# Loading the first tile of a rotary-embedding kernel in four pieces ahead of its tables, and storing the last tile in four pieces

## The chip, the core and the metric

The kernel runs on one core of one Trainium2 chip. The metric is the time of one execution on the device in microseconds (us), as the median of several executions. A profile is a separate, recorded execution with its own time; the span is the part of it from the first to the last instruction.

The core has a matrix engine (TensorE, "PE" in the profile), a vector engine (VectorE, "DVE"), a scalar engine (ScalarE, "ACT"), GpSimd ("POOL") and SyncE ("SP"). In this kernel SP only issues transfers. The transfers themselves are carried by 16 DMA engines. An engine whose name ends in q in the profile, such as SPq, is its instruction queue: issuing a transfer or waiting there is not counted as busy time.

## The reference

The reference applies a rotary position embedding to x of shape 16 x 512 x 1024, in float32. Each row of 1024 is 16 heads of 64, and each head is cut into two halves of 32. The cosine and sine tables have one row of 32 for each of the 512 positions.

```python
x = x.reshape(batch, seq, num_heads, head_dim)
x1, x2 = x[..., :half_dim], x[..., half_dim:]
cos, sin = cos[None, :, None, :], sin[None, :, None, :]
rotated = np.concatenate([x1 * cos - x2 * sin, x1 * sin + x2 * cos], axis=-1)
```

So 32 MiB are read, 32 MiB are written, and the arithmetic is two products and a sum for each element.

## The kernel before

**Tiling.** Two batches make a tile: 64 partitions for each, 128 in all, with R = 8 consecutive positions (rows of 1024) on each partition. A tile is 128 partitions by 8192 numbers, 4 MiB, with 32 KB on each partition. There are NT = 8 tiles. The pool `xin` holds NB = 5 of them, and the result is written over the tile itself, so that a tile's buffer is loaded, rotated in place and stored from.

**Tables.** The tables are loaded as `tabs` (64 partitions, 256 numbers for sine and 256 for cosine; lines 61 and 62). Three matrix products (lines 88 to 90) spread them over the 128 partitions into PSUM, as `sns_ps` (sine with both signs) and `cos_ps`, and ScalarE copies them to SBUF as `sns` and `cost` (lines 94 and 95). VectorE reads the PSUM copies and GpSimd reads `sns`.

**One tile (`compute`).** Rows 0 and 1 are single rows: the swapped halves are multiplied by the sine into B (line 121; row 0 on GpSimd, row 1 on VectorE), the row by the cosine in place (line 131, VectorE), and the matrix engine adds the two through an identity matrix (lines 136 and 137), from where ScalarE copies the sum back into the tile (line 138). Rows 2 and 3, 4 and 5, 6 and 7 go as pairs: GpSimd makes T (line 126), VectorE makes the cosine product pp (line 142) and adds both into the tile (line 143).

**Order of the transfers.** The schedule is written by hand, and each engine runs its instructions in the order of the program. All transfers are issued by SP, on one queue: sine, cosine, the first tile in two halves of 2 MiB (lines 63 and 64), and tiles 1 to 4 whole (line 68). Then tiles 0, 1 and 2 are stored when they are done (line 148); tiles 5, 6 and 7 are loaded into the buffers that these stores free (line 68 again); tiles 3 and 4 are stored (line 152), then 5 and 6 (line 156), and the last tile in two halves (lines 157 and 158). A store waits for its rows on VectorE and ScalarE; the second half of the last tile waits for VectorE's last instruction.

```python
nc.sync.dma_start(out=tabs[:, 1], in_=sinv)
nc.sync.dma_start(out=tabs[:, 0], in_=cosv)
nc.sync.dma_start(out=x_tiles[0][:, :H], in_=xv[0][:, :H])
nc.sync.dma_start(out=x_tiles[0][:, H:], in_=xv[0][:, H:])
```

The full kernel follows.

Of the kernel before, what the change touches and what calls it, by code (L numbers as in the profile page):

```python
# [7 lines left out]
FP32 = mybir.dt.float32  # L8
# [4 lines left out]
def kernel(  # L13
# [8 lines left out]
    nc = tc.nc  # L22
    P = nc.NUM_PARTITIONS
    batch, seq, dim = x.shape
# [7 lines left out]
    R = seq // HP  # L32
    NT = batch // BP
# [5 lines left out]
    xv = x.rearrange("b (p r) d -> (b p) (r d)", r=R)  # L39
    xv = xv.rearrange("(t p) f -> t p f", p=P)  # L40
    ov = out.rearrange("b (p r) h d -> (b p) (r h d)", r=R)
    ov = ov.rearrange("(t p) f -> t p f", p=P)
    cosv = cos.rearrange("(p r) j -> p (r j)", r=R)
    sinv = sin.rearrange("(p r) j -> p (r j)", r=R)

    fixed = ctx.enter_context(tc.tile_pool(name="fixed", bufs=1))
    xin = ctx.enter_context(tc.tile_pool(name="xin", bufs=NB))
# [6 lines left out]
    ctx.enter_context(tc.manual_schedule())  # L54


    tabs = fixed.tile([HP, 2, R * half], FP32, name="tabs")
    x_tiles = [None] * NT
    x_tiles[0] = xin.tile([P, R * dim], FP32, name="x_sb")
    H = R * dim // 2  # L60
    nc.sync.dma_start(out=tabs[:, 1], in_=sinv)
    nc.sync.dma_start(out=tabs[:, 0], in_=cosv)
    nc.sync.dma_start(out=x_tiles[0][:, :H], in_=xv[0][:, :H])
    nc.sync.dma_start(out=x_tiles[0][:, H:], in_=xv[0][:, H:])

    def load(t):
        x_tiles[t] = xin.tile([P, R * dim], FP32, name="x_sb")
        nc.sync.dma_start(out=x_tiles[t], in_=xv[t])

    for t in range(1, NB):  # L70
        load(t)

# [4 lines left out]
        out=ident, in_=ident, compare_op=ALU.not_equal, fill=1.0,  # L77
# [35 lines left out]
    def compute(t):  # L113
        xt = x_tiles[t]
        ts = {}
        bs = {}

        for r in PEROWS:
            B = bpool.tile([P, dim], FP32, name="B")
            eng = nc.vector if r == PEROWS[-1] else nc.gpsimd  # L120
            eng.tensor_tensor(out=B, in0=swapped(xt, r, 1), in1=snsb(sns_ps if eng is nc.vector else sns, r, 1),  # L121
                              op=ALU.mult)
            bs[r] = B
        for r0 in PAIRS:
            T = tpool.tile([P, 2 * dim], FP32, name="T")
            nc.gpsimd.tensor_tensor(out=T, in0=swapped(xt, r0, 2), in1=snsb(sns, r0, 2), op=ALU.mult)  # L126
            ts[r0] = T

        for r in reversed(PEROWS):
            xr = view(xt, r, 1)  # L130
            nc.vector.tensor_tensor(out=xr, in0=xr, in1=cosb(cos_ps, r, 1), op=ALU.mult)  # L131
            for c in range(2):
                ps = prow.tile([P, dim // 2], FP32, name="ps")
                xc = xr[:, c * dim // 2:(c + 1) * dim // 2]
                bc = bs[r][:, c * dim // 2:(c + 1) * dim // 2]
                nc.tensor.matmul(out=ps, lhsT=ident, rhs=xc, start=True, stop=False)  # L136
                nc.tensor.matmul(out=ps, lhsT=ident, rhs=bc, start=False, stop=True)  # L137
                nc.scalar.copy(out=xc, in_=ps)  # L138
        for r0 in PAIRS:
            pp = ppair.tile([P, 2 * dim], FP32, name="pp")  # L140
            xr = view(xt, r0, 2)
            nc.vector.tensor_tensor(out=pp, in0=xr, in1=cosb(cos_ps, r0, 2), op=ALU.mult)  # L142
            nc.vector.tensor_tensor(out=xr, in0=ts[r0], in1=pp, op=ALU.add)  # L143

    for t in range(NB):
        compute(t)
        if t < NT - NB:
            nc.sync.dma_start(out=ov[t], in_=x_tiles[t])
    for t in range(NB, NT):
        load(t)  # L150
    for t in range(NT - NB, NB):
        nc.sync.dma_start(out=ov[t], in_=x_tiles[t])
    for t in range(NB, NT):
        compute(t)
        if t < NT - 1:
            nc.sync.dma_start(out=ov[t], in_=x_tiles[t])
    nc.sync.dma_start(out=ov[NT - 1][:, :H], in_=x_tiles[NT - 1][:, :H])
    nc.sync.dma_start(out=ov[NT - 1][:, H:], in_=x_tiles[NT - 1][:, H:])


# [33 lines left out]
```

## Time and profile before

| quantity | before |
|---|---|
| time, median of 3 runs | 164.61 us (164.56 to 164.94) |
| time of the profiled execution | 164.86 us |
| its span | 162.7 us |
| VectorE busy | 137.7 us (85%) |
| GpSimd busy | 127.1 us (78%) |
| TensorE busy (modelled ends) | 77.5 us (48%) |
| ScalarE busy | 21.0 us (13%) |
| packet time of the one data queue, as a share of 16 engines' span | 97.0% |
| bytes moved | 67.25 MB, 413 GB/s over the span |
| transfers issued by SP | 20 |

The busy times are sums over the span; the shares are averages over stages. The profile also shows for every transfer the time from its issue to its landing, and for stretches of the span the DMA engines' busy share. In the view by stretches a packet is counted whole in the stretch in which it ends, so that a share can be over 1.00 in one row and under it in the next. Besides, the trace holds a record of every packet of a transfer, with its start, its length in time and its bytes. A packet of a tile is one partition's share of a transfer: 32,768 bytes for a whole tile and 16,384 for a half.

### The profile page before, as it was taken

How to read it: one execution, taken by the hardware profiler on the slowest of the kernel's cores; microseconds unless marked ns; L12 is line 12 of the kernel's file. 1: busy time of each engine (PE TensorE's matmuls, PEld its weight loads, DVE VectorE, ACT ScalarE, POOL GpSimd, SP SyncE). 2: the span in 40 equal slices, each digit the busy share in tenths (PEclk: the TensorE clock that was granted, in tenths of full speed). 3: DMA queues.
4: the chain of work that ended last, by engine and by line, in shares of the span. 5: the costliest groups of instructions: out<-in, count | busy, mean ns of one | idle time of the engine just before them, and what ended most of it. 6: DMA issues, size and time to landing. Idle time of an engine off the chain costs nothing. (4 is left out here: it accounts for less than half of the span.)

```text
span 162.7 us, 575 instructions
## 1 busy us (share of the span) xinstructions
PE 77.5 (48%) x134; PEld 32.3 (20%) x134; DVE 137.7 (85%) x75; ACT 21.0 (13%) x35; POOL 127.1 (78%) x38
## 2 busy tenths in 40 slices
PE   2409910499019920894059701990089205990000
PEld 2204400243013400341024201330034002330000
DVE  1067999999999999999999999999999999999100
ACT  3200310013101210022002300121004100131000
POOL 1069999999998799959995999779995999590000
PEclk9999997559855995589557995699659975598555
DMA  4999989999899998999999999989989989999992
GB/s 101 387 447 467 435 387 500 403 395 508 387 403 371 443 459 387 475 427 403 467 413 411 467 411 427 475 387 459 443 387 459 443 387 492 411 411 415 439 427 121
DMA packets 2753, 67.25 MB, mean 413 GB/s; under 512 B 320, under 2 KB 448, under 8 KB 448
## 3 DMA queue, kind: packets, MB, share of 16 engines
q1 hardware_dynamic: 2752, 67.24, 97.0%
q14 instruction: 1, 0.01, 0.0%
HBM read 33.69 MB, written 33.55 MB: 413 GB/s over the span
## 5 line engine op out<-in xcount | busy, mean ns | idle before, releaser
L126 POOL TENSOR_TENSOR T<-x_sb,sns 128x2048 f32<-128x2048 f32 x24 | 108.3, 4532 | 10.4 <-DVE x_sb L143 10.4
L136 PE MATMUL ps<-x_sb,ident 128*128 128x512 f32 x64 | 44.4, 783 | 65.7 <-issue 41.4
L143 DVE TENSOR_TENSOR x_sb<-T,pp 128x2048 f32<-128x2048 f32 x24 | 54.9, 2287 | 3.4 <-POOL T L126 1.0
L142 DVE TENSOR_TENSOR pp<-x_sb,cos_ps 128x2048 f32<-128x2048 f32 x24 | 55.0, 2293 | 0.6
L137 PE MATMUL ps<-B,ident 128*128 128x512 f32 x64 | 40.1, 713 | 0.0
L138 ACT COPY x_sb<-ps 128x512 f32<-128x512 f32 x32 | 18.8, 586 | 121.7 <-PE ps L137 120.6
L136 PEld LDWEIGHTS ps<-x_sb,ident 128*128 128x128 f32 x64 | 15.1, 251 | 87.8 <-issue 81.0
L121 POOL TENSOR_TENSOR B<-x_sb,sns 128x1024 f32<-128x1024 f32 x8 | 18.8, 2350 | 8.3 <-DMA x_sb<-in_x_dram 8.3
L137 PEld LDWEIGHTS ps<-B,ident 128*128 128x128 f32 x64 | 15.4, 240 | 21.8 <-issue 21.8
L131 DVE TENSOR_TENSOR x_sb<-x_sb,cos_ps 128x1024 f32<-128x1024 f32 x16 | 18.8, 1218 | 0.5
L121 DVE TENSOR_TENSOR B<-x_sb,sns_ps 128x1024 f32<-128x1024 f32 x8 | 9.7, 1215 | 7.7 <-DMA x_sb<-in_x_dram 7.7
L88 PE MATMUL sns_ps<-tabs,sel 64*128 64x256 f32 x2 | 1.2, 696 | 3.1 <-DMA tabs<-in_sin_dram 3.1
L94 ACT ACT_TABLE_LOAD x1 | 1.3, 1283 | 0.7 <-PEq L175 0.7
L81 DVE COPY sel<-ident 64x64 f32<-64x64 f32 x1 | 0.2, 186 | 1.3 <-POOL ident L76 1.3
L88 PEld LDWEIGHTS sns_ps<-tabs,sel 64*128 64x128 f32 x2 | 0.5, 306 | 3.1 <-issue 3.1
L89 PE MATMUL sns_ps<-tabs,sel 64*128 64x256 f32 x2 | 1.1, 631 | 0.0
L90 PE MATMUL cos_ps<-tabs,sel 64*128 64x256 f32 x2 | 1.1, 631 | 0.0
L94 ACT COPY sns<-sns_ps 128x512 f32<-128x512 f32 x1 | 0.6, 586 | 3.2 <-PE sns_ps L89 3.2
L89 PEld LDWEIGHTS sns_ps<-tabs,sel 64*128 64x128 f32 x2 | 0.7, 333 | 0.2
L90 PEld LDWEIGHTS cos_ps<-tabs,sel 64*128 64x128 f32 x2 | 0.7, 333 | 0.2
L75 POOL MEMSET ident<- 128x128 f32 x1 | 0.2, 205 | 0.3 <-POOLq L175 0.3
L95 ACT COPY cost<-cos_ps 128x256 f32<-128x256 f32 x1 | 0.4, 373 | 0.3 <-PE cos_ps L90 0.3
(7 smaller groups left out, 1.1 us busy)
## 6 DMA issues: line engine op xcount, KB each, us to landing
x_sb<-in_x_dram SPq DMA_DIRECT2D x7, 4096.0 KB, 29.8
out_dram<-x_sb SPq DMA_DIRECT2D x7, 4096.0 KB, 27.5
x_sb<-in_x_dram SPq DMA_DIRECT2D x2, 2048.0 KB, 9.6
out_dram<-x_sb SPq DMA_DIRECT2D x2, 2048.0 KB, 10.1
tabs<-in_sin_dram SPq DMA_DIRECT2D x1, 64.0 KB, 2.2
tabs<-in_cos_dram SPq DMA_DIRECT2D x1, 64.0 KB, 2.3
```

The source lines that it names most:

```text
L88: nc.tensor.matmul(out=sns_ps[:, :, 1, :], lhsT=sel[:, 0, :], rhs=sin3, start=True, stop=True)
L89: nc.tensor.matmul(out=sns_ps[:, :, 0, :], lhsT=sel[:, 1, :], rhs=sin3, start=True, stop=True)
L90: nc.tensor.matmul(out=cos_ps.rearrange("p r j -> p (r j)"), lhsT=sel[:, 0, :], rhs=tabs[:, 0], start=True, stop=True)
L94: nc.scalar.copy(out=sns, in_=sns_ps)
L121: eng.tensor_tensor(out=B, in0=swapped(xt, r, 1), in1=snsb(sns_ps if eng is nc.vector else sns, r, 1), op=ALU.mult)
L126: nc.gpsimd.tensor_tensor(out=T, in0=swapped(xt, r0, 2), in1=snsb(sns, r0, 2), op=ALU.mult)
L131: nc.vector.tensor_tensor(out=xr, in0=xr, in1=cosb(cos_ps, r, 1), op=ALU.mult)
L136: nc.tensor.matmul(out=ps, lhsT=ident, rhs=xc, start=True, stop=False)
L137: nc.tensor.matmul(out=ps, lhsT=ident, rhs=bc, start=False, stop=True)
L138: nc.scalar.copy(out=xc, in_=ps)
L142: nc.vector.tensor_tensor(out=pp, in0=xr, in1=cosb(cos_ps, r0, 2), op=ALU.mult)
L143: nc.vector.tensor_tensor(out=xr, in0=ts[r0], in1=pp, op=ALU.add)
```

## The change

The order of the first transfers, the queue of the two tables and the cutting of the first load and of the last store change; arithmetic, tiles and buffers stay. The first tile is loaded ahead of the tables in four pieces of two rows each (128 partitions by 2048 numbers, 1 MiB, 8,192 bytes on each partition). The tables are issued by ScalarE, on its own queue. The last tile is stored in four pieces of the same size. There are 24 transfers instead of 20: 22 issued by SP and 2 by ScalarE.

```diff
+    x_tiles = [None] * NT
+    def load(t, pieces=1):
+        x_tiles[t] = xin.tile([P, R * dim], FP32, name="x_sb")
+        n = R * dim // pieces
+        for i in range(pieces):
+            nc.sync.dma_start(out=x_tiles[t][:, i * n:(i + 1) * n], in_=xv[t][:, i * n:(i + 1) * n])
+
+    def store(t, pieces=1):
+        n = R * dim // pieces
+        for i in range(pieces):
+            nc.sync.dma_start(out=ov[t][:, i * n:(i + 1) * n], in_=x_tiles[t][:, i * n:(i + 1) * n])
+
+    load(0, pieces=4)
     tabs = fixed.tile([HP, 2, R * half], FP32, name="tabs")
-    nc.sync.dma_start(out=tabs[:, 1], in_=sinv)
-    nc.sync.dma_start(out=tabs[:, 0], in_=cosv)
-    nc.sync.dma_start(out=x_tiles[0][:, :H], in_=xv[0][:, :H])
-    nc.sync.dma_start(out=x_tiles[0][:, H:], in_=xv[0][:, H:])
+    nc.scalar.dma_start(out=tabs[:, 1], in_=sinv)
+    nc.scalar.dma_start(out=tabs[:, 0], in_=cosv)
...
     for t in range(NB, NT):
         compute(t)
-        if t < NT - 1:
-            nc.sync.dma_start(out=ov[t], in_=x_tiles[t])
-    nc.sync.dma_start(out=ov[NT - 1][:, :H], in_=x_tiles[NT - 1][:, :H])
-    nc.sync.dma_start(out=ov[NT - 1][:, H:], in_=x_tiles[NT - 1][:, H:])
+        store(t, pieces=4 if t == NT - 1 else 1)
```

On the compute engines the order of instructions is the same as before. On ScalarE the two issues stand ahead of the activation-table load that was its first instruction. Transfers share eight completion semaphores in turn, and as these are dealt out anew, two loads get a wait that they did not have: the load of tile 3 waits for the landing of the sine table, and that of tile 4 for the landing of the first piece of tile 0.

More of the change, by code (lines that the diff above doesn't have):

```diff
@@ L54 @@
     ctx.enter_context(tc.manual_schedule())
-    tabs = fixed.tile([HP, 2, R * half], FP32, name="tabs")
[L58 to L63, printed above, removed]
-    nc.sync.dma_start(out=x_tiles[0][:, H:], in_=xv[0][:, H:])
-    def load(t):
-        x_tiles[t] = xin.tile([P, R * dim], FP32, name="x_sb")
-        nc.sync.dma_start(out=x_tiles[t], in_=xv[t])
+    x_tiles = [None] * NT
+    Q = 2 * dim
+    def load(t, pieces=1):
[8 more added lines that the diff above has]
+    load(0, pieces=4)
+    tabs = fixed.tile([HP, 2, R * half], FP32, name="tabs")
+    nc.scalar.dma_start(out=tabs[:, 1], in_=sinv)
+    nc.scalar.dma_start(out=tabs[:, 0], in_=cosv)
     for t in range(1, NB):
@@ L147 @@
         if t < NT - NB:
-            nc.sync.dma_start(out=ov[t], in_=x_tiles[t])
+            store(t)
     for t in range(NB, NT):
@@ L151 @@
     for t in range(NT - NB, NB):
-        nc.sync.dma_start(out=ov[t], in_=x_tiles[t])
+        store(t)
     for t in range(NB, NT):
         compute(t)
-        if t < NT - 1:
-            nc.sync.dma_start(out=ov[t], in_=x_tiles[t])
-    nc.sync.dma_start(out=ov[NT - 1][:, :H], in_=x_tiles[NT - 1][:, :H])
-    nc.sync.dma_start(out=ov[NT - 1][:, H:], in_=x_tiles[NT - 1][:, H:])
+        store(t, pieces=4 if t == NT - 1 else 1)
 _INS = ['x', 'cos', 'sin', 'num_heads']
```

## The prediction

> **What bounds the kernel.** I read the page's busy shares first, then the 40 slices and the queue.
>
> ```profile
> PE 77.5 (48%) x134; PEld 32.3 (20%) x134; DVE 137.7 (85%) x75; ACT 21.0 (13%) x35; POOL 127.1 (78%) x38
> ...
> DMA  4999989999899998999999999989989989999992
> ...
> q1 hardware_dynamic: 2752, 67.24, 97.0%
> ```
>
> No compute engine is above 85%, while the DMA engines are full in every slice but the first and the last. Next comes the order of SP's issues (start, length, line).
>
> ```profile
> 0.73 0.54 SPq L61 DMA_DIRECT2D tabs<-in_sin_dram  x1
> 1.33 0.57 SPq L62 DMA_DIRECT2D tabs<-in_cos_dram  x1
> 1.96 0.58 SPq L63 DMA_DIRECT2D x_sb<-in_x_dram  x1
> ...
> 146.89 0.33 SPq L157 DMA_DIRECT2D out_dram<-x_sb  x1
> 151.29 0.33 SPq L158 DMA_DIRECT2D out_dram<-x_sb  x1
> ```
>
> By the lines' own views the halves L157 and L158 land 9.8 and 10.3 us after issue, so at 156.7 and 161.6: 4.9 us apart, though issued 4.4 apart. The last half is not late because VectorE was: it stood in line. The wait view says the same of SP's end, and shows what compute waits for at the start:
>
> ```profile
> SPq L189 <- DMA out_dram<-x_sb: 10.0, 1, 10.0
> ```
> ```profile
> DVE B L121 <- DMA x_sb<-in_x_dram: 7.7, 1, 7.7
> ```
>
> Short stretches show the two edges (columns: stretch, length, five engines' busy time, clock, DMA share, GB/s).
>
> ```profile
> 2.00:2.50 0.50, 0.00 (x0) 0.00 (x0) 0.00 (x0) 0.01 (x1) 0.00 (x0) 1.00 0.34 115
> 2.50:3.00 0.50, 0.00 (x0) 0.00 (x0) 0.00 (x0) 0.00 (x0) 0.00 (x0) 1.00 0.54 96
> 3.00:3.50 0.50, 0.39 (x1) 0.42 (x2) 0.00 (x0) 0.00 (x0) 0.00 (x0) 1.00 2.36 510
> ...
> 159.50:160.00 0.50, 0.00 (x0) 0.00 (x0) 0.00 (x0) 0.00 (x0) 0.00 (x0) 0.50 0.32 131
> 160.00:160.50 0.50, 0.00 (x0) 0.00 (x0) 0.00 (x0) 0.00 (x0) 0.00 (x0) 0.50 0.08 33
> ```
>
> Between 2 and 3 us only tables move, with holes; between 3 and 160 the engines are full. The packet records are finer: the first packet of x starts at 3.19 us, 16 packets are in flight from then to 159.7, 15 engines are done by 160.3 and the last at 161.25. So the span is: the start of the x stream, plus the work of one DMA engine (4.2 MB), plus about 1.4 us from its last packet to the last instruction. Compute counts only where it makes that stream run dry.
>
> **Prices, from the packet records.** One packet holds its engine for 1.213 us at 32 KB, 0.611 at 16 KB, 0.046 at 1 KB (the tables) and 0.009 for a 4-byte completion. That is 0.0367 us per KB plus some 0.009 a packet, so 8 KB should take 0.310; a lone 8 KB instruction fetch at 83.5 us took 0.309. Each engine carries 8 packets of a 128-partition transfer and 4 of a table.
>
> **Part 1: the tables leave SP's queue.** Their issues fill 0.735 to 1.962, and x is now issued first. The sine table, issued at 0.735, had its first packet at 2.06; the first x packet, issued at 1.962, at 3.19: 1.2 to 1.3 us from issue to packet. So x can start at 2.06: **-1.13 us**. The bounds: if ScalarE's sine issue takes its turn ahead, x is where cosine was (issue 1.34, first packet 2.70): -0.49; if both go ahead, 0. ScalarE begins its first instruction at 0.733 in this trace and SP at 0.735, so the trace doesn't say who comes first if they must take turns; its back-to-back issues on one engine show no turns between two. I take the two as parallel and keep 0 as the far end.
>
> **Part 2: the tables' packets.** Before, they ran while x was still on its way; now they run beside it. An engine has 8 packets of 0.046 and 2 completions of 0.009: **+0.39 us** if the engine is full. The first x packets took 0.83 to 1.51 us instead of 0.611, some 0.8 us lost on each engine once; table packets might fit into that for nothing, so the other end is 0. I take the full price, since everywhere else in the stream an extra packet shows as time.
>
> **Part 3: quarters for halves**, twice. A tile costs an engine 32 packets of 0.310 instead of 16 of 0.611: 9.92 - 9.78 = 0.14. Two more completions with their gaps of 0.006: 0.03. Both tiles: **+0.34 us**. Between the two halves of the first tile the records show no hole, only the 0.015 us of a completion. The lower end is 0, as a smaller packet can't carry the same bytes cheaper. The upper: 8 KB fetches before the span took 0.42 to 0.55, so 0.11 more on 64 packets, +7 us; that is far off, on idle engines, and the fetch inside the stream gives 0.309.
>
> The Trainium skill speaks against this part. "DMA: Bandwidth & Descriptors", section "Anatomy of one DMA — SWDGE (gpsimd) path", gives each DMA some 2.0 us of fixed cost beside its bytes, which for four more DMAs would be an estimated +8 us. The rows above disagree for queued transfers, as the halves follow each other within 0.015 us; the page's figure is for another issue path and for a DMA by itself.
>
> **Part 4: earlier compute.** The first quarter (rows 0 and 1) should land near 2.06 + 0.8 + 8 x 0.31 + 0.35 = 5.7 instead of 9.5. Sine landed at 3.0 and VectorE could start 2.15 us later (three matrix products queued); with packets interleaved I put sine near 4.5 and VectorE's start near 6.7 instead of 9.56. Worth **nothing**: the stream is full, and compute's lead at the stores only grows. What covers it: the next half-store's packets started at 150.2 (median engine), and it was issued at 146.89, 1.3 us of latency, so 2.0 us were left; at the last half (155.0 against 151.29) 2.45. With quarters the first piece, which still waits for ScalarE's copies of row 0, is the tight one: its turn comes 0.4 us sooner, 1.6 left, if compute did not start earlier at all.
>
> **Part 5: the last store in quarters.** Pieces are ready in order; the last, ready at 151.3, has its turn near 157.1. No gain, since the end is the queue's. The lagging engine gains nothing either: each engine carries its own partitions.
>
> **Part 6: new waits.** SP's loads of tiles 3 and 4 wait for sine and for the first quarter, some 5.7 us; behind them in SP's order is the first store, not due before 24. By then tiles 0 to 2, 29 us of work, are queued. ScalarE's table load (1.28 us) starts about 1.2 later and ends near 3.3, before its first copy. Both 0.
>
> **Sum:** -1.13 + 0.39 + 0.34 = **-0.40 us**. The profiled execution goes from 162.65 to 162.25 in span, and, with the 2.2 us outside it unchanged, from 164.86 to 164.46; its time is 0.25 above the median of 164.61, which goes to **164.2**.
>
> **Rivals.**
>
> *The tables hide in the slow first packets.* The 0.39 falls away: -0.79, 163.8. For it: 0.8 us per engine is there to fill. Against: whether an engine serves a second queue in that time isn't shown, as all data is on one.
>
> *The two queues take turns at issue,* tables first, so that x doesn't start earlier, or by 0.49: -0.49 + 0.2 (cosine alone in the stream) + 0.34 = +0.05, up to +0.34; 164.6 to 165.0. It is the case in which the change doesn't do what it says. For it: first issues take 0.54 to 0.58 each, which leaves turns visible.
>
> *The tables starve (slower).* If their packets stand behind all the quarters, sine lands near 2.06 + 0.8 + 9.92 + 0.35 = 13.1 and VectorE starts at 15.3, 5.7 late. From 1.6 us late on (a start after 11.2, sine after 9.0) each us shows at the end: 5.7 - 1.6 - 0.4 = +3.7, 168.3. Against: x is cut in small packets, and with turns by packet sine's four would wait 4 x 0.31.
>
> The skill's page "DMA: Bandwidth & Descriptors", section "Queues, rings and completion order", has each engine take queues in turn packet by packet; no transfer of this trace shows it.
>
> *The lagging engine.* One engine ended 1.35 us after the median. Its delays came once right after the instruction fetch at 83.5 us (a 32 KB packet of 1.776) and once near 111 (1.719). Landing on different engines they cost 0.5 less; with the splits dearer than computed, 0.5 to 1 more.
>
> **How the numbers follow.** Forecast 0.32; hidden tables 0.20; turns at issue 0.25; starving 0.05; lagging engine or dearer pieces 0.18, more of it slower. A difference of 0.3%, 0.49 us, is about what a measurement of this kernel can tell from no change. Faster takes hidden tables, a part of the forecast (its edge is 0.1 us away) and a kinder lag: 0.36. Slower takes starving, most of dearer pieces and the upper end of turns: 0.17. The range reaches from hidden tables with 0.2 of spread (163.6) to turns at issue at their worst (165.0); starving and the worst pieces are outside.
>
> **What would show it.** Right: the first x packet near 2.1 us; DMA full from then on; 8 KB packets of 0.31; VectorE's first line-126 instruction (B, 121 before) near 6.7, and yet the last packet only about 0.4 us sooner. The first step is wrong if the DMA share begins as late as before; the fourth if a stretch after 55 us has idle DMA engines; the whole argument if the end moves with VectorE's start.

## The result, and the profile after

The changed kernel takes 163.11 us (162.99 to 163.42, four runs) against 164.59 for the kernel before in the same comparison: a ratio of 0.9906, 95% interval 0.9882 to 0.9930, so 1.48 us faster. The forecast was 0.40 us faster, 164.2, with a range from 163.6; the direction was right and the size was not. The profiled execution took 162.99 us, its span is 160.97 us (before: 164.86 and 162.65).

The page after, slices and queues (share of 16 engines last):

```profile
DMA  5999999999999999999999999999999999999994
...
q1 hardware_dynamic: 3168, 67.11, 97.6%
q10 hardware_dynamic: 160, 0.13, 0.3%
```

The stream is as full as before, and the tables have a queue of their own (q10). The timeline of the first issues (start, length), ScalarE's and then SP's:

```profile
0.73 0.54 ACTq L73 DMA_DIRECT2D tabs<-in_sin_dram  x1
1.30 0.61 ACTq L74 DMA_DIRECT2D tabs<-in_cos_dram  x1
```
```profile
0.73 6.12 SPq L64 DMA_DIRECT2D x_sb<-in_x_dram  x8
```

Both engines issue from 0.73 us on, side by side. In the kernel before, no data had moved between 1.5 and 2 us:

```profile
1.50:2.00 0.50, 0.00 (x0) 0.00 (x0) 0.34 (x3) 0.50 (x1) 0.00 (x0) 1.00 0.00 0
```

With the change, at the two edges:

```profile
1.50:2.00 0.50, 0.00 (x0) 0.00 (x0) 0.34 (x3) 0.06 (x1) 0.00 (x0) 1.00 1.10 164
2.00:2.50 0.50, 0.00 (x0) 0.00 (x0) 0.00 (x0) 0.50 (x1) 0.00 (x0) 1.00 0.44 98
2.50:3.00 0.50, 0.00 (x0) 0.00 (x0) 0.00 (x0) 0.50 (x1) 0.00 (x0) 1.00 0.89 360
...
158.50:159.00 0.50, 0.00 (x0) 0.00 (x0) 0.00 (x0) 0.00 (x0) 0.00 (x0) 0.50 0.28 115
159.00:159.50 0.50, 0.00 (x0) 0.00 (x0) 0.00 (x0) 0.00 (x0) 0.00 (x0) 0.50 0.15 66
159.50:160.00 0.50, 0.00 (x0) 0.00 (x0) 0.00 (x0) 0.00 (x0) 0.00 (x0) 0.50 0.00 0
```

Data moves before 2 us, and the engines run dry about a microsecond sooner. What the first operations wait for has changed as well (waits of compute, then of SP's queue):

```profile
DVE B L126 <- ACT sns L99: 7.0, 1, 7.0
PE sns_ps L93 <- DMA tabs<-in_sin_dram: 6.2, 1, 6.2
```
```profile
SPq L191 <- DMA out_dram<-x_sb: 9.0, 4, 2.4
```

Compute now waits for the tables and not for x (the matrix products wait for sine, ScalarE's copy for them, and VectorE for that copy): sine landed 5.3 us after its issue instead of 2.2. SP still ends by waiting for stores.

**Where the time went.** The span can be taken apart with the packet records. Here *loss* is packet time above what a packet of that size normally takes (1.213 us at 32 KB, 0.912 at the 24 KB of e12, 0.611, 0.309, 0.046 or 0.009), summed and divided by 16 engines. The kernels before and after were each profiled twice (the second time as e1 and e16 below); *start* is the median start of the first 16 x packets, *end* that of the 16 engines' last completions, *last* the end of the last packet of all:

```
                   start  loss 0-4  4-16  16-48  48-56 us | end, median  last  to span's end
before              3.34    0.75    0.11   0.02   0.76    |  159.91    161.25     1.40
before again (e1)   3.30    0.70    0.04   0.01   0.95    |  160.09    160.87     1.41
after               1.88    0.50    0.49   0.11   0.07    |  158.80    159.81     1.16
after again (e16)   1.91    0.37    0.43   0.11   0.14    |  158.65    159.71     1.16
```

Between 48 and 56 us the load of tile 4 gives way to the first store. Means of the pairs: start -1.43; loss, 1.67 to 1.11, -0.56. Of this, 0.12 lay before in the packets of the tables themselves, ahead of the stream, so that -0.44 is left for the stream; table packets +0.39; quarters +0.28 at 0.309 for a packet of 8 KB; from the last packet to the span's end -0.25. That makes -1.45; the spans differ by 1.55 (162.47 to 160.92), so 0.10 has no account.

The landings show the loss at the first store without this sum: from the load of tile 3 to that of tile 4 (means of the 16 engines) it took 10.46 and 10.66 us before, and 9.76 and 9.83 with the change.

### The profile page after: what moved, and what is told of

Same layout as the page of the kernel before. It is cut to its first block, busy times and chain, and to the rows that moved or that the text cites. A ratio compares the mean times of both kernels' runs of the same rounds, so it can differ in the third digit from the quotient of the medians.

```text
span 161.0 us, 581 instructions
## 1 busy us (share of the span) xinstructions
PE 78.3 (49%) x134; PEld 32.3 (20%) x134; DVE 137.8 (86%) x75; ACT 21.0 (13%) x35; POOL 127.1 (79%) x38
```

## The experiments

All ratios are to the kernel before, with 95% intervals.

**e1 and e16: both kernels again.** No edit.

> The kernel before, unchanged, profiled once more. In its first profile the first x packet started at 3.19 us, each DMA engine lost 0.76 us between 48 and 56 us (slow packets where the load of tile 4 gives way to the first store), and the last data packet ended at 161.25; in the changed kernel these were 1.74, 0.07 and 159.81. Chance theory: the loss at 48 to 56 us comes and goes, so here it is under 0.3 us and the span near 162.0 us. Rival, the loss belongs to the order of transfers before the change: it is 0.6 to 0.9 us again and the span 162.5 to 162.8. Ratio to before 1.000 either way, interval within 0.003.

Measured: ratio 1.0016 (1.0001 to 1.0031), loss 0.95 us, span 162.28. The same kernel can come out 0.2% apart here. The loss recurs, so chance is an unlikely account of it.

> The changed kernel, unchanged. x starts at 1.7 to 1.9 us, loss at the first store under 0.3, span 160.7 to 161.3, ratio 0.988 to 0.993.

Measured: 162.81 us, ratio 0.9876 (0.9849 to 0.9903), loss 0.14, span 160.87. The gain recurs, if anything larger.

**e2: the front alone.**

```diff
-        store(t, pieces=4 if t == NT - 1 else 1)
+        store(t, pieces=2 if t == NT - 1 else 1)
```

> The change without its tail: the last tile is stored in two halves as before. Stream theory (the span is the start of the x stream plus one engine's work): the start stays at 1.7 to 1.9 us and one tile's quarter packets (0.17 us) are saved, so span 160.7 to 161.0, ratio 0.989 to 0.991. Rival, the quarter stores shorten the end: about a third or more of the gain is lost, span 161.4 or more, ratio 0.993 or more.

Measured: 0.9912 (0.9891 to 0.9932), span 160.94. The front brings all that can be measured.

**e3: the tail alone.** The kernel before, with the last tile stored in four pieces.

> The kernel before with the last tile stored in four pieces, nothing else. Stream theory: the end is the queue's, the packets cost 0.17 us more, span 162.6 to 162.9, ratio 1.000 to 1.002. Rival, the quarter stores shorten the end: span 162.1 or less, ratio 0.997 or less.

Measured: 1.0009 (0.9993 to 1.0026), span 162.95, loss 0.93. The quarter stores bring nothing, as forecast.

**e4: the same order on one queue.**

```diff
 x_tiles[0] quarter 0 on SP
+nc.sync.dma_start(out=tabs[:, 1], in_=sinv)
+nc.sync.dma_start(out=tabs[:, 0], in_=cosv)
 x_tiles[0] quarters 1 to 3 on SP
-nc.scalar.dma_start(out=tabs[:, 1], in_=sinv)
-nc.scalar.dma_start(out=tabs[:, 0], in_=cosv)
```

> The changed kernel with the tables back on SP's queue, right behind the first quarter of tile 0; last store in four pieces. Stream theory: x starts at 1.7 to 2.1 us as it does with two queues, since it is the first transfer; the first quarter covers the two table issues; span 160.7 to 161.1, ratio 0.989 to 0.992, and sine lands before 5.5 us. Rival, the second queue brings the gain (issues side by side): x starts no earlier than 2.06 and the queue shows a hole while SP issues the tables, span 161.4 or more, ratio 0.993 or more.

Measured: 0.9935 (0.9904 to 0.9966), start 1.89, span 161.11. The start is the change's. The queue isn't needed for it; that x goes first is. The ratio lies just inside the rival's range, as two of the five executions took 164.1 and 164.2 us; its interval covers both ranges, so the start and the span decide.

**e5 to e8: what takes the loss away?** Four fronts, all with the last store in halves: e5 is the kernel before with tile 0 in quarters, e6 with tile 0 whole; e7 is e2 with tile 0 in halves; e8 is e7 with the tables on SP behind them.

> The kernel before, but tile 0 loaded in four pieces; tables still first on SP, last store in halves. What the last runs left open is the loss where the load of tile 4 gives way to the first store: 0.76, 0.95 and 0.93 us for each DMA engine with the front of before, 0.07 to 0.19 with x first. Front theory (the loss belongs to tables ahead of x): 0.7 to 1.0 us again, span 162.4 to 162.9, ratio 1.000 to 1.003. Pieces theory (four pieces take it away): under 0.3, span 161.6 to 162.1, ratio 0.996 to 0.998. Count theory (it comes where exactly 64 packets and completions of an engine, as before, stand ahead of the first store in the queue; here 82): under 0.3, as pieces.

> The kernel before, but tile 0 loaded in one piece; tables first on SP. Front theory and pieces theory: loss 0.7 to 1.0 us, span 162.2 to 162.6, ratio 0.998 to 1.001. Count theory (55 packets and completions ahead of the first store): loss under 0.3, span 161.4 to 161.9, ratio 0.994 to 0.997. Compute starts about 5 us later than before (the whole tile lands near 13.9 us), which the lead at the stores does not cover fully (2 us were left at the last tile): that may add 2 to 3 us to the end in all theories; the loss is then read from the packets alone.

> x first in two halves on SP, tables on ScalarE's queue, last store in halves: the order of the change without its pieces. Start of x 1.7 to 1.9 us in all theories. Front theory and count theory (54): loss under 0.3, span 160.6 to 161.0, ratio 0.988 to 0.991. Pieces theory: loss 0.7 to 1.0, span 161.3 to 161.7, ratio 0.992 to 0.995.

> x first in two halves, the tables behind it on SP's queue, last store in halves; 64 packets and completions ahead of the first store, as before. The tables land after the second half, near 12.5 us, so compute starts near 15 us, 5 late, and the end may be 2 to 3 us later for that in all theories. Front theory: loss at the first store under 0.3. Count theory and pieces theory: 0.7 to 1.0.

Measured, with VectorE's first start:

```
      ratio (interval)             start  loss 48-56  VectorE  span
e5    0.9973 (0.9960 to 0.9986)    3.34     1.05       7.07    162.11
e6    1.0063 (1.0040 to 1.0085)    3.33     1.01      14.39    163.40
e7    0.9924 (0.9894 to 0.9953)    1.88     0.05      11.56    161.73
e8    1.0189 (1.0164 to 1.0215)    1.88     0.03      16.58    165.95
```

Pieces do not decide (e5 in four pieces loses, e7 in two does not), nor does the count of packets (e8 has the 64 of before). These four left tables ahead of x as the cause. In e8 the loss is gone only at the first switch: 0.90 us for each engine go near 79 us, where the loads resume, and 0.85 near 109, at the second switch to stores. e5 is a little faster than before although it starts and loses alike, and was expected at 1.000 to 1.003; its last engine ends 0.70 us behind its median instead of 1.07, which is no more than such profiles differ by. The four also show what pieces are for: in e6 and e8 compute starts late, and the end is late for it. In e7 it is so in part: its last half store lands 5.46 us behind the first, for 4.86 of packets, and its span missed the expected 160.6 to 161.0. In e6 the stream runs dry at the last tile:

```profile
148.00:150.00 2.00, 2.00 (x6) 0.76 (x4) 1.90 (x2) 0.59 (x1) 2.00 (x1) 1.00 0.95 410
150.00:152.00 2.00, 0.49 (x2) 0.00 (x0) 1.97 (x2) 0.59 (x1) 1.27 (x1) 1.00 0.18 74
152.00:154.00 2.00, 0.00 (x0) 0.00 (x0) 1.90 (x2) 0.00 (x0) 0.00 (x0) 0.65 1.11 467
```

The hole before 152 us (share 0.18) is the first half store not yet ready. Between the completions of tile 6 and of that half lie 6.53 us for 4.86 us of packets: 1.67 lost.

**e9 to e11: first, late, or ahead on the other queue.** e9 is e2 with an unused 64 KB copy of the cosine table first on SP. e10 is e4 with the last store in halves, and e11 is e2, each with x held back by

```diff
+nc.vector.memset(x_tiles[0][:, :dim], 0.0)
```

> The change with the last store in halves, and one more transfer: a copy of the cosine table (64 KB, unused) goes first on SP, ahead of x. So x starts near 2.4 to 2.7 us instead of 1.75. Theory small-first (the loss at the first store comes when table rows are the first thing that the DMA engines carry): loss 0.7 to 1.0 us for each engine between 48 and 56 us, span 162.1 to 162.7, ratio 0.996 to 1.000. Theory start-time (the loss comes when x starts near 3.2 us and not near 1.8): somewhere between none and all. Null theory (the order does not matter, the loss was chance in eleven profiles): under 0.3 or over by chance. Without the loss span 161.5 to 161.9, ratio 0.992 to 0.996.

> All on SP: first quarter of x, the tables, the other quarters, last store in halves; but the first quarter waits for a VectorE write into its first row (which it then overwrites), so that x is still first on the DMA engines and starts near 3 us instead of 1.75. Small-first theory: loss at the first store under 0.3, span 161.9 to 162.4, ratio 0.995 to 0.999. Start-time theory: loss 0.7 to 1.0, span 162.7 to 163.2, ratio 1.000 to 1.004.

> The change with the last store in halves, but the first quarter waits for the same VectorE write, so that the tables (ScalarE's queue) are carried ahead of x, which starts near 3 us on SP's queue. Small-first theory, if what counts is the first thing on the DMA engines: loss 0.7 to 1.0, span 162.3 to 162.9, ratio 0.998 to 1.002. Small-first theory, if what counts is the first thing on SP's queue: loss under 0.3, span 161.5 to 162.1, ratio 0.993 to 0.997. Start-time theory: loss 0.7 to 1.0.

Measured:

```
      ratio (interval)             start  loss 4-16  loss 48-56  span    table packets start
e9    0.9906 (0.9873 to 0.9939)    2.76     0.30       0.23      162.21  2.07 to 6.44
e10   0.9987 (0.9963 to 1.0011)    3.12     0.59       0.24      162.83  5.82 to 6.71
e11   0.9929 (0.9904 to 0.9954)    3.25     0.06       0.79      161.87  2.06 to 3.65
```

Small-first falls with e9, start-time with e10. (e9's profiled execution was its slowest, 164.42 us; the other five took 163.10 to 163.37.) In both, table packets run while x is already flowing; in e11 they are nearly through when it starts, and the loss is back. That suggested another cause: what matters may be not what goes first but whether small packets run inside the stream of x.

e11 fits neither expectation in time: with that loss and a start at 3.25 it was expected no faster than 0.998, and all five of its executions took 163.77 to 164.02, against a median of 165.03 for the kernel before. Neither the start nor the loss explains these; it stays open. What a late start costs is read more directly from e10 against e4, which have the same order of loads: x starts 1.23 us later, and the median engine ends 1.18 us later (159.85 against 158.67).

**e12: a candidate.** e4's order with the other six rows in one piece and the last store in halves.

> A candidate: all on SP, first quarter of tile 0 (rows 0 and 1), the tables, then the other six rows in one piece, last store in halves. It has 0.3 us less of packet time than the change (fewer pieces, nothing taken in turns). x starts at 1.75, no loss at the first store by the small-first and start-time theories: span 160.5 to 160.9, ratio 0.988 to 0.991. Compute starts near 7.3 us, then waits for the six rows, which land near 13, so its lead is about that of before; if that is too little, the last half store shows a hole and the span is 161 or more.

Measured: 0.9902 (0.9863 to 0.9940), span 161.01, loss at the first store 0.52 where none was expected. In time nothing tells it from the change. VectorE's first start, 8.72, was later than expected, and between the first half store and the completion of tile 6 lie 5.16 us instead of 4.86, a small hole.

**e13 to e15: inside or not.** e13 puts two unused 64 KB copies of the tables behind the halves of tile 0 of the kernel before, e14 the same two behind the load of tile 4. e15 is e2 without the loads of the tables, which hold a constant instead.

```diff
 e13, behind nc.sync.dma_start(out=x_tiles[0][:, H:], in_=xv[0][:, H:])
+nc.sync.dma_start(out=spare[:, 1], in_=sinv)
+nc.sync.dma_start(out=spare[:, 0], in_=cosv)
 e15
-nc.scalar.dma_start(out=tabs[:, 1], in_=sinv)
-nc.scalar.dma_start(out=tabs[:, 0], in_=cosv)
+nc.vector.memset(tabs, 0.5)
```

> The kernel before with two more transfers of 64 KB (copies of the tables, unused), on SP behind the two halves of tile 0. Tables ahead of x as before, x starts at 3.2 us. Inside theory: loss at the first store under 0.3, span 161.8 to 162.3, although there is 0.4 us more of packets. Order theory: loss 0.7 to 1.05, span 162.6 to 163.1.

> The same two unused transfers, but behind the load of tile 4, so right ahead of the first store in the queue. Inside theory, if what small packets shift among the engines is what helps: loss at the switch under 0.4, split over packets around the two transfers. Order theory: 0.7 to 1.05, span 162.6 to 163.1.

> The change with the last store in halves and without the loads of the tables: the tables are set to a constant by VectorE, so the table loads are left out. x starts at 1.75 us and no small packets run at all. Inside theory: loss 0.7 to 1.05, so the span is about what it is with the tables inside: 160.6 to 161.2 (0.4 to 0.7 us of table packets and turns less, 0.7 of loss more). Order theory: loss under 0.3, span 160.0 to 160.5.

Measured:

```
      ratio (interval)             start  loss 4-16  loss 48-56  span
e13   0.9985 (0.9968 to 1.0003)    3.35     0.47       0.05      162.96
e14   1.0028 (1.0008 to 1.0048)    3.38     0.04       0.71      162.97
e15   0.9938 (0.9918 to 0.9958)    1.86     0.01       1.01      161.45
```

e13 has the tables ahead of x like the kernel before, and the loss at the first store is gone. e15 has x first like the change, and the loss is there. So the order theory falls, and inside stands, on one profile of each. When compute starts does not sort the profiles either: VectorE's first start is 5.51 to 14.39 us in those with the loss and 7.09 to 16.58 in those without, and e13 (9.59) starts like the kernel before (9.55). e13 missed its expected span (161.8 to 162.3), because the loss is not simply removed: most of it is paid where the small packets run. In every profile with small packets inside the early stream 0.30 to 0.59 us are lost between 4 and 16 us and 0.03 to 0.24 at the first store (0.52 in e12); in every one without, 0.01 to 0.11 and 0.71 to 1.05. e14 came out as the order theory had it. One reading, made after the fact, is that its packets come too late: the slow packets start from 51.2 to 51.7, the small ones from 52.9 on. And e15, with 0.13 MB less to load, has the longer span, 161.45 (160.6 to 161.2 was expected) against 160.94 in e2; the two ratios overlap at their edges, so no gain from it is seen.

## Why the prediction was wrong

**What bounds the kernel** was read rightly: the stream of x sets the span. In the change VectorE started at 8.86 us instead of 6.7 as forecast, and nothing followed from it.

**The step that failed is the sum.** It let only the start, the tables' packets and the quarters change, and held the rest of the stream and its end fixed. The span fell by 1.55 us instead of 0.40. By the account above, 0.44 of the missing 1.15 are losses in the stream that shrank, 0.30 the start, 0.25 the time behind the last packet, 0.06 the quarters, and 0.10 is open. The direction rests on the forecast's own terms, which as measured give -0.76 (start -1.43, tables +0.39, quarters +0.28). The rest of the gain, some 0.8, came from places that it held fixed: that the change did better than forecast by this much was luck.

**Part 1, the start, was mis-sized**: -1.13 forecast, -1.43 measured. I took the delay from issue to first packet from the sine table (1.33 us). x as first transfer needs 1.0: issued at 0.74, first packet at 1.74. It isn't the coming first that does it, since in e10, issued at 1.96, its first packet came at 2.98, and in e9 the table in first place kept 1.34. The delay is better counted from the end of the issue instruction. The first quarter's issue takes 0.38 us, the first half's before took 0.58, and x's first packet came 0.63 to 0.65 us behind that end in the change, in e10, in e9 and before; for a table in first place it was 0.78.

**Part 2 was right on the packets and wrong on what they do to the stream.** Their own time is 0.39 us as forecast. But the trace of before had 0.76 us of slow packets at the first store, and the forecast had no term for them. With tables inside the stream 0.75 us go there, and 0.38 come back between 4 and 16 us and 0.1 behind that (means of the pairs). In all, losses up to 56 us fall by 0.56, in the stream by 0.44. So with their own 0.39 the tables gain nothing by running inside, as e13 shows too: it adds two such transfers, and its ratio is 0.9985. The rival in which the tables hide in the slow first packets named another place for a gain of like size. The losses in the first 4 us did shrink (0.72 to 0.44, means of two, 0.12 of it the tables' own), but no table packet ran then in the change: the first came at 4.69.

**Part 3** holds: 8 KB packets took 0.309 us, which makes 0.28 of the 0.34. The fixed cost of each DMA that the Trainium skill gives ("DMA: Bandwidth & Descriptors", "Anatomy of one DMA — SWDGE (gpsimd) path"), an estimated +8 us for four more, does not appear in this queued stream: e3, with two transfers more than before, has 1.0009.

**Parts 4 to 6** hold in what they are worth: the lead covers compute, though sine landed near 6.0 and not at 4.5; the tail alone gives nothing (e3); and no stretch inside the stream shows the new waits. The cover was larger than I read: e6's start is 4.8 us later than before, and 1.67 us of that shows, where my lead of 2.0 would have left 2.8.

**The rivals.** Turns at issue fall: SP and ScalarE issue at the same time. Starving falls, but in part it is true: sine, issued at 0.73, had its first packet at 4.69, when 106 of the first quarter's 128 packets had ended, where a table going first has it at 2.06. It is not a wait for the whole first transfer: in e7 the first came at 5.46, with 64 of the first half's 128 packets ended. In e9 sine, on the same queue, landed within 2.8 us of its issue, so no fixed wait explains it. The rule of the Trainium skill ("DMA: Bandwidth & Descriptors", "Queues, rings and completion order"), by which an engine takes queues in turn packet by packet, fits what follows and not the beginning: cosine's 64 packets start from 5.30 to 7.16 among 69 of x, but sine's 64 came within 0.57 us among 22 of x. The page counts a packet as several descriptors, and no record here shows whether the profile's packets are the page's. The lagging engine is undecided and small: it ends 1.07 us behind the median before and 1.04 after, means of two.

**What stays open.** Why small packets inside the stream take away the loss at the first store isn't shown. A shift of the 16 engines against each other is a guess, as the records do not name the engine. How far apart they run does not tell: at 48 us the 16 packets under way had started within 0.40 us of each other before, 0.38 in e15, 0.47 with the change and 0.38 in e2. Nor is it known why e8, without the loss at the first store, has 0.90 and 0.85 at later switches. Nor is it settled why the time from the last packet to the span's end is 1.16 us with the change and 1.40 and 1.41 before; in the other kernels it is 1.16 to 1.44, without a pattern that I can see.

## What to carry to other kernels

In a kernel whose transfers keep all DMA engines full, put the first big transfer ahead of everything small: its delay is time on the end (1.23 us of it gave 1.18 in e10 against e4), and the tables' is not while compute has a lead. Read that lead at the stores before cutting pieces; pieces only pay if they keep it. And when the engines are full, sum the packets' losses by stretch: a term that is there before the change can leave with it.

## What the hardware showed unexpectedly

- The first switch from loads to stores cost each engine 0.71 to 1.05 us in eight profiles and 0.03 to 0.24 in nine with small packets earlier in the stream (0.52 in one). The span without 0.13 MB of loads was 161.45 us (e15), with them 160.94 (e2).
- A transfer of 128 partitions by 8 KB had its first packet 1.0 us after the start of its issue, one of 64 partitions by 1 KB 1.33 us; from the end of the issue it was 0.63 and 0.78.
- The tables on the second queue got no packet until 4.69 us, when 106 of the first quarter's 128 packets had ended; beside a first half of 16 KB packets (e7) it was 5.46 us and 64 of 128.
